# The gated heads' half of the output projection as seven block products instead of eight

## The chip, the cores and the metric

The kernel runs on one core of one Trainium2 chip. The metric is the device time of one execution in microseconds (us). The engines are TensorE (PE: matrix products, its weight loads are listed apart as PEld), VectorE (DVE), ScalarE (ACT), GpSimd (POOL) and SyncE (SP). PE writes to PSUM, eight banks of 128 x 512 float32; the others copy from there into SBUF. Transfers between SBUF and the chip's DRAM are issued by SP's queue or by POOL's queue and are carried by 16 DMA engines. Each engine takes its instructions strictly in the order of its own list.

## The reference, cut to what matters

A decoder layer on a sequence of 1024 rows, 1024 wide. After a norm the input is multiplied by `w_in`; eight heads of differential softmax attention give `oa` (1024 x 1024) and four heads of gated linear attention give `ob` (1024 x 1024). Each is normed and gated. Then comes the output projection:

```python
    ob = rms_norm(ob, gla_g).astype(x.dtype)
    ob = ob.reshape(B, S, GLA_WIDTH) * jax.nn.silu(gb)

    y = jnp.einsum('bse,ed->bsd', jnp.concatenate([oa, ob], axis=-1), w_out)
    return x + rms_norm(y, post_g)
```

`y` is therefore a sum of two products of 1024 x 1024 matrices: `oa` with the upper half of `w_out`, and `ob` (the gated heads' half) with the lower half. The change touches only how the second one is computed.

## The kernel before

**Precision.** Every float32 operand of a product is split into `hi` (rounded by a cast on ACT) and `lo` (the rest, by a subtraction on DVE), and each product is three matmuls: hi by hi, lo by hi, hi by lo. A split is thus one ACT and one DVE instruction on a 128 x 512 tile, and two transfers where the parts are stored.

**First stage, the input projection** (from the start to about 630 us). It already runs as seven products of blocks (`order`, steps (pair of columns, product number)); `go` takes one step after another: `prepare` splits the weights of the step that lies up to three steps ahead (`prepare(i + a)` for a = 0 to 3, into a ring of `NRING` = 5 tiles), `multiply` issues 12 matmuls (24 for wide ones), and `step` moves the sums on. Beside each step two things are worked off: `wo_step` loads one 128 x 512 tile of `w_out` (`wo_raw`), splits it (L584, L586) and stores the parts in DRAM (`wod`), 32 tiles in all; and from step (12, 5) on, `fill` advances `gla`, the gated heads, by one of its pieces. `gla` handles one head and half of the rows at a time (eight in all). Its last piece scales and gates the 2 x 128 x 512 result `o`, splits it at once and stores both parts in `mixe`.

**Second stage, attention and output projection** (about 630 to 925 us). `merge` interleaves three streams in the order of planned times: `all_scores` (scores and softmax, PE tile `sc`), `all_values` (transposes `wtr`, products `po`) and `out_early` (the output projection, PE tile `ypart`). What `merge` settles is the order of PE's list, which is pinned; the order on the other engines is a scheduler's. The loads of a head's keys and queries (`load_qk`, L875 and L878) are issued by SP when the head before has released the tiles.

`out_early` first makes the gated half: for each of 8 row tiles `st` and 2 column halves `dh`, 8 products of 128 x 128 x 512 over `e`, each three matmuls, that is 8 x 2 x 8 x 3 = 384 matmuls. ACT copies the sum from PSUM (`y_tile`, L1256) and SP stores it in DRAM (`yd`). The weights of this half, 16 tiles of 512 KB, are loaded once by POOL's queue before the stage starts (`weights(e)`, L910); the left sides come with `mix(st)`, two loads of 512 KB for each row tile. The last row tile waits until seven results of attention are stored. Then the first four attention heads' part is made in the same way, and POOL adds each sum to `yd` by an accumulating transfer (L1314).

**End** (from about 925 us): the last heads' part, the final norm and the stores.

Of the kernel before, what the change touches and what calls it, by code (L numbers as in the profile page):

```python
# [31 lines left out]
def hymba_kernel(  # L32
# [49 lines left out]
    gla_g = const.tile([P, 2], F32, name="gla_g")  # L82
# [15 lines left out]
    mixe = tc.dram_tile([NT, 2, P, 8, P], F32, name="mixe")  # L98
    wod = [tc.dram_tile([2, P, D], F32, name=f"wo{e}_d") for e in range(2 * D // P)]
# [84 lines left out]
    raws = {}  # L184

    def load_raw(p, halves=(0, 1)):
        if p >= len(pairs):
            return
        c0 = pairs[p][2]
        for kh in halves:  # L190
            if kh not in raws.setdefault(p, {}):
                r = ap.tile([P, HB, 256], F32, tag="raw", name="w_raw", bufs=4)
                rows = slice(kh * 512, kh * 512 + 512)
                sp.dma_start(r, w_in[0, rows, c0 : c0 + 256].rearrange("(k p) c -> p k c", p=P))
                raws[p][kh] = r
# [381 lines left out]
    wo_todo = [(e % 16, dh) for e in range(8, 24) for dh in range(2)]  # L577
    wo_open = []

    def wo_step(n):  # L580
        if n in (1, 6) and wo_open:
            e, dh, raw = wo_open.pop()
            hi = t_c("wo_hi", F32R)
            act.copy(hi, raw)  # L584
            lo = raw.bitcast(F32R)
            dve.tensor_tensor(lo, raw, fp(hi), ALU.subtract)  # L586
            for t, src in enumerate((hi, lo)):
                sp.dma_start(wod[e][t][:, cols(dh)], fp(src))
        if n in (2, 4) and wo_todo:
            e, dh = wo_todo.pop(0)  # L590
            raw = ap.tile([P, 512], F32, tag="t4", name="wo_raw", bufs=1)
            sp.dma_start(raw, w_out[0, e * P : (e + 1) * P, cols(dh)])
            wo_open.append((e, dh, raw))

    def go(n):
        for _ in range(n):
            i = made[0]
            if i == len(order):
                return
            made[0] = i + 1  # L600
            for a in range(4):
                prepare(i + a)
            step(i)
            if order[i][0] > EARLY and not (wide(order[i][0]) and order[i][0] % 2):
                wo_step(order[i][1])
            if fill and next(fill[0], 0) == 0:
                fill.pop(0)
# [114 lines left out]
    sp.dma_start(gla_g, gla_norm_g[0].rearrange("(t p) -> p t", p=P))  # L722
    lam4 = t_c("lam4").rearrange("p (a b) -> p a b", b=128)[:, :, :64]
# [19 lines left out]
    def gla_loads(g, half):  # L743

        if g < GLA_HEADS and (g, half) not in loaded:
# [3 lines left out]
            qd = kp.tile([P, 512], F32, tag="q1", name="gqd")  # L749
# [7 lines left out]

    def gla(g):

        u = None  # L760
        for half in range(2):
            cs = cols(half)
            kq, v, qd = gla_loads(g, half)
            gates = kp.tile([P, 2, 512], F32, tag="ks1", name="gg")
            yield
# [16 lines left out]
            act.copy(kn, pk)  # L782
            for t in range(2):
                sp.dma_start(gates[:, t], gg_d[g][t, :, cs])
            yield
            yield
            yield
            us = [u]
            for m in range(2):
# [8 lines left out]
                for i in range(min(2, NT - 1 - n)):  # L798
                    u1, u = u, ap.tile([P, 256], F32, tag="gu", name="gu", bufs=5)
# [46 lines left out]
            m_hi = gates.bitcast(F32R)  # L846
            for t in range(2):
                dve.scalar_tensor_tensor(
                    o[:, t], o[:, t], gla_g[:, t : t + 1], r, ALU.mult, ALU.mult
                )  # L850
                dve.tensor_tensor(o[:, t], o[:, t], gates[:, t], ALU.mult)
                act.copy(m_hi[:, t], o[:, t])
                m_lo = o[:, t].bitcast(F32R)
                dve.tensor_tensor(m_lo, o[:, t], fp(m_hi[:, t]), ALU.subtract)
                for i, src in enumerate((m_hi[:, t], m_lo)):
                    sp.dma_start(
                        mixe[half * 4 : half * 4 + 4, i, :, 2 * g + t, :].rearrange("s p c -> p s c"),
                        fp(src).rearrange("p (s c) -> p s c", c=P),
                    )
            yield  # L860

# [24 lines left out]
    fill.append(chain(*(gla(g) for g in range(GLA_HEADS))))  # L886
# [13 lines left out]
    def weights(e):  # L900
        i = e % 8
        wo[e] = [
            hw.tile(
                [P, D], F32R, tag=f"{('h11', 'h12', 's1', 'h22')[i // 2]}_{n}{i % 2}", name=f"wo_{n}"
            )
            for n in ("hi", "lo")
        ]
        engine = sp if e < E else pool
        for t in range(2):
            ins = engine.dma_start(fp(wo[e][t]), wod[e][t])  # L910
            if e >= E:
                tc.keep_in_program_order(ins)

    n_mix = [0]
# [8 lines left out]
    def mix(st):  # L923

        part = mix_tiles()
        for t in range(2):
            ins = sp.dma_start(fp(part[t]), mixe[st, t])
            if st < 2:
                tc.keep_in_program_order(ins)
        return part  # L930

    for e in range(E, E + 6):
        weights(e)
    go(2)
    mix0 = mix(0)
    go(3)
    weights(E + 6)
    weights(E + 7)
# [315 lines left out]
    def y_tile(ps):  # L1254
        y = smp.tile([P, 512], F32, tag="yst", name="yst", bufs=2)
        act.copy(y, ps)  # L1256
        return y

    def out_early():

        part = mix0
        ps = [y_bank(0, dh, "ypart") for dh in range(2)]
        for e in range(E, E + 8):
            yield 1.0
            if e == E:
                nxt = mix(1)
            for dh in range(2):
                times(ps[dh], part, E, dh, e, E + 7)
            yield 1.0
        for dh in range(2):  # L1270
            sp.dma_start(yd[0][dh], y_tile(ps[dh]))
        for st in range(1, NT - 1):
            part, nxt = nxt, mix(st + 1)
            rows = slice(ENDS[st - 1] * P, ENDS[st - 1] * P + P)
            sp.dma_start(out[0, rows, :], x[0, rows, :])
            for dh in range(2):
                ps = y_bank(st, dh, "ypart")
                for e in range(E, E + 8):
                    times(ps, part, E, dh, e, E + 7)
                    yield 0.69  # L1280
                sp.dma_start(yd[st][dh], y_tile(ps))

        yield lambda: len(stored) >= 7
        part = nxt
        ps = [y_bank(NT - 1, dh, "ypart") for dh in range(2)]
        raws_o = [load_mix(st, 0, 4) for st in ENDS[:3]]
        for e in range(E, E + 8):
            for dh in range(2):
                times(ps[dh], part, E, dh, e, E + 7)
                yield 0.69  # L1290
            if e < E + 4:
                weights(e - E)
            if e == E + 6:
                nxt = mix_part(ENDS[0], 0, 4, raws_o.pop(0))
        for dh in range(2):
            kept = sp.dma_start(yd[NT - 1][dh], y_tile(ps[dh]))
        for n, st in enumerate(ENDS):
# [11 lines left out]
            for dh in range(2):  # L1309
# [4 lines left out]
                pool.dma_start(yd[st][dh], y_tile(ps), accum_op=ALU.add)  # L1314
# [61 lines left out]
    def seed(st, dh, b, yp):  # L1376
# [3 lines left out]
        pin(b not in Y, act.copy(ps, yp))  # L1380

    def last_times(st, dh, part, e):
# [17 lines left out]
        [-6.0, T + LAG + 20, 16.0 + 14 * 5.52 + 16 * 2.76 + 11.8, out_early()],  # L1400
# [125 lines left out]
```

## Time and profile before

| | before |
|---|---|
| time, median of 3 runs (lowest to highest) | 980.24 us (978.34 to 980.25) |
| the profiled execution's own time | 979.08 us |
| its span, first to last instruction | 977.4 us |
| granted TensorE clock | 0.999 |
| busy: PE, DVE, ACT, POOL | 956.7, 735.4, 600.5, 142.9 us |
| moved by DMA | 220.45 MB, mean 226 GB/s |

A group line of the profile reads: source line, engine, operation, output tile <- input tiles, shape, xcount | busy us in all, mean ns of one | idle time of the engine just before them, and what ended it. A line of stages ("windows") reads: stretch in us, then for PE, PEld, DVE, ACT and POOL the busy us with the count of instructions, the granted clock, the mean busy share of the 16 DMA engines, and GB/s. In a list of waits the numbers are us in all, times, and the longest. The profile's DMA line for a queue gives packets, MB and the share of the 16 engines' time that its packets took.

### The profile page before, as it was taken

To read this page: it belongs to the slowest core of one execution; us is meant where nothing else is said; L and a number is where in the kernel's file an instruction comes from. 1 tells how busy PE (TensorE), PEld (TensorE's weight loads), DVE (VectorE), ACT (ScalarE), POOL (GpSimd) and SP (SyncE) were. 2 spreads that over 40 slices of the span, in tenths; PEclk is the share of its full clock that TensorE was granted. 3 is DMA by queue.
4 is the path that set the end of the run, shared out by engine and by line. 5 is a ranking of instruction groups with operands and counts; after the bars stand their busy time and mean duration, and the time that the engine had idled before them with its cause. 6 is when DMAs were issued, how large, how long until landed. Compare 5 with 4: busy or idle time off the path is not lost.

```text
span 977.4 us, 15766 instructions
## 1 busy us (share of the span) xinstructions
PE 956.7 (98%) x5338; PEld 830.4 (85%) x5338; DVE 735.4 (75%) x1452; ACT 600.5 (61%) x1164; POOL 142.9 (15%) x158
## 2 busy tenths in 40 slices
PE   5999999999999999999999999999999999999997
PEld 5998988888889998999888888878888888888785
DVE  6887597789866667686786876487888888898554
ACT  8742455487357455454665775366776687887773
POOL 4300000000000010000200002121322222443321
PEclk9999999999999999999999999999999999999999
DMA  9432446656774868897987866987656669994677
GB/s 345 151 110 91 139 135 205 231 179 225 238 247 162 264 187 286 254 294 229 293 259 243 273 202 191 407 269 272 197 186 228 240 199 344 340 294 105 151 208 147
DMA packets 152593, 220.45 MB, mean 226 GB/s; under 512 B 17104, under 2 KB 83664, under 8 KB 152416
## 3 DMA queue, kind: packets, MB, share of 16 engines
q1 hardware_dynamic: 146176, 203.71, 64.1%
q0 software_dynamic: 6336, 15.73, 7.0%
q8 instruction: 42, 0.69, 0.3%
q14 instruction: 39, 0.32, 0.1%
HBM read 133.93 MB, written 88.60 MB: 228 GB/s over the span
## 4 chain that ended last, share of the span: by engine, by line
PE 95%; DVE 2%; ACT 1%; DMA 1%; issue 1%; POOL 0%; SPq 0%; DVEq 0%; ACTq 0%; POOLq 0%
PE x L117 24%; PE y L117 15%; PE z L117 15%; PE ypart L117 13%; PE sc L117 7%; PE po L117 5%; PE yps L117 4%; PE wtr L120 3%; PE gpo L117 3%; PE kv L117 1%; PE gkl_ps L117 1%; PE pa L117 1%; DMA x<-in_x_dram 1%; PE xT L120 1%; DVE s_lo L548 0%
## 5 line engine op out<-in xcount | busy, mean ns | idle before, releaser
L315 ACT CAST w<-w_raw 128x512 fp32r<-128x512 f32 (+1 forms) x164 | 112.4, 688 | 94.7 <-PE y L117 44.1
L316 DVE TENSOR_TENSOR w<-w_raw,w 128x512 fp32r<-128x512 f32 (+1 forms) x164 | 126.7, 774 | 50.1 <-ACT w L315 43.3
L1049 ACT ACTIVATE p<-p,stt 128x896 f32<-128x896 f32 (+7 forms) x128 | 99.3, 777 | 36.7 <-DVE stt L1039 33.9
L427 ACT COPY s<-x 128x512 f32<-128x512 f32 x84 | 49.1, 585 | 84.4 <-PE x L117 84.3
L775 POOL TENSOR_SCALAR_AFFINE_SELECT gan<-gan 128x512 f32<-128x512 f32 x8 | 16.5, 2060 | 485.4 <-ACT gan L774 449.8
L296 DVE TENSOR_TENSOR w_raw<-w_raw 128x512 f32<-128x512 f32 (+1 forms) x96 | 75.9, 791 | 13.9 <-DMA w_raw<-in_w_in_dram 12.6
L1039 DVE CUSTOM_DVE_ANT_0 p<-sc,maskt 128x512 f32<-128x512 f32 (+3 forms) x128 | 74.3, 585 | 14.5 <-PE sc L117 13.3
L117 PE MATMUL ypart<-wo_hi,m_hi 128*128 128x512 f32 x192 | 79.5, 414 | 0.1
L117 PE MATMUL y<-h_hi,w 128*128 128x512 f32 x320 | 79.6, 391 | 0.0
L117 PE MATMUL z<-s_hi,w 128*128 128x512 f32 x320 | 79.6, 391 | 0.0
L117 PE MATMUL x<-s_hi,w 128*128 128x512 f32 x320 | 79.6, 391 | 0.0
L1055 POOL TENSOR_SCALAR p<-p,stt,lam 128x1024 f32<-128x1024 f32 (+3 forms) x64 | 56.2, 879 | 146.9 <-DVE stt L1054 141.9
L117 PE MATMUL ypart<-wo_hi,m_lo 128*128 128x512 f32 x192 | 75.5, 393 | 0.0
L117 PE MATMUL ypart<-wo_lo,m_hi 128*128 128x512 f32 x192 | 75.4, 393 | 0.0
L117 PE MATMUL sc<-k,q 128*128 128x512 f32 (+1 forms) x192 | 69.0, 363 | 1.3 <-DVE stt L1039 1.2
L117 PEld LDWEIGHTS x<-s_hi,w 128*128 128x128 f32 x320 | 59.7, 188 | 12.2
L117 PEld LDWEIGHTS y<-h_hi,w 128*128 128x128 f32 x320 | 59.6, 188 | 12.2
L117 PEld LDWEIGHTS z<-s_hi,w 128*128 128x128 f32 x320 | 59.5, 188 | 12.0
L117 PE MATMUL sc<-ks,q 128*128 128x512 f32 (+1 forms) x192 | 66.1, 347 | 0.0
L1097 ACT CAST wt_hi<-wtr 128x512 fp32r<-128x512 f32 (+1 forms) x80 | 42.7, 534 | 24.6 <-PE wtr L120 23.8
L1098 DVE TENSOR_TENSOR wt_lo<-wtr,wt_hi 128x512 fp32r<-128x512 f32 (+1 forms) x80 | 50.7, 633 | 8.6 <-ACT wt_hi L1097 8.0
L1058 DVE SCALAR_TENSOR_TENSOR p<-p,stt,p 128x1024 f32<-128x1024 f32 (+3 forms) x64 | 52.1, 814 | 4.1 <-POOL p L1055 3.9
(226 smaller groups left out, 2247.7 us busy)
## 6 DMA issues: line engine op xcount, KB each, us to landing
w_raw<-in_w_in_dram SPq DMA_DIRECT2D x56, 512.0 KB, 4.7
wo_raw<-in_w_out_dram SPq DMA_DIRECT2D x32, 256.0 KB, 3.0
wo_d<-wo_hi SPq DMA_DIRECT2D x32, 256.0 KB, 2.8
wo_d<-wo_raw SPq DMA_DIRECT2D x32, 256.0 KB, 3.8
q<-q_d SPq DMA_DIRECT2D x32, 256.0 KB, 4.7
k<-k_d SPq DMA_DIRECT2D x32, 256.0 KB, 5.7
ks<-k_d SPq DMA_DIRECT2D x64, 128.0 KB, 6.2
v<-v_d SPq DMA_DIRECT2D x16, 512.0 KB, 7.0
```

The costliest lines, as they stand in the source:

```text
L117: tc.keep_in_program_order(pe.matmul(*a, **k))
L120: tc.keep_in_program_order(pe.transpose(dst, src, ident))
L296: dve.tensor_tensor(dst, a, b, ALU.subtract)
L315: act.copy(w[0], src)
L316: dve.tensor_tensor(w[1], src, fp(w[0]), ALU.subtract)
L427: act.copy(b[k], ps)
L1039: ins = dve.tensor_tensor_reduce(p[:, a:e], sc[:, : e - a], maskt[:, NZ + P - (e - a) :] if last else maskt[:, : e - a], 1.0, 3e38 if i == ...
L1049: act.activation(p[:, :n], p[:, :n], AF.Exp, bias=st[:, m : m + 1], scale=-1.0, accum_out=st[:, 2 + m : 3 + m],)
L1055: pool.tensor_scalar(p1[:, :n], p1[:, :n], st[:, 5:6], lam, ALU.mult, ALU.mult)
L1058: dve.scalar_tensor_tensor(p0[:, :n], p0[:, :n], st[:, 4:5], p1[:, :n], ALU.mult, ALU.subtract)
L1097: act.copy(hi[:, :n], pt[:, :n])
L1098: dve.tensor_tensor(lo[:, :n], pt[:, :n], fp(hi[:, :n]), ALU.subtract)
```

## The change

Write the gated half as a product of 2 x 2 blocks of 512 rows or columns, left A (rows in two halves, columns by heads 0-1 and 2-3) and right W. Seven products of sums of blocks replace the eight products (the recipe that `order` uses in the input projection already). In detail:

- `out_early` runs over `U`, 28 entries (product n, row tile i of 128): each is 4 x 3 = 12 matmuls into a bank. Products 6 and 7 go on top of product 1 in the same bank, and 3 on top of 5, each after the bank has been copied out. That makes 28 x 12 = 336 matmuls.
- Each entry's bank is copied out by ACT: 28 copies. Sixteen of the results are stored in `yd` by SP, and sixteen are added to it by POOL's accumulating transfers (one entry of product 7 serves both).
- The four weight blocks that are sums are made in DRAM: SP copies a block of `w_out` to `wsd`, POOL adds another to it (16 copies, 16 accumulating transfers of 256 KB). `wo_step` splits 16 tiles of these beside 12 plain blocks and 16 tiles of the other half (before: 32 tiles), now one job every second step at most, with up to three raw tiles in flight; a spare half of the gated heads' `gqd` tile is one of them.
- The left sides that are sums are made in DRAM too (`lefts`): SP stores `o` (8 transfers of 512 KB), POOL adds (8 accumulating transfers). The split of `o` itself moves into the next piece (`gla_tails`) and is done for six of the eight results; 10 tiles of the sums are split by `wo_step`, and the last 6 by `late_left` beside the first products of the second stage.
- The left sides come in with one load of 512 KB for each entry (28 loads, four entries ahead); the weights of products 2, 4, 1 and 6 come by POOL's queue at the start (16 loads of 512 KB), those of 7, 5 and 3 by SP during the products (12 loads of 512 KB).
- Column half 1 of `y` is held with its sign turned, which `activation` with a scale undoes.

By the lists of instructions of the two kernels, PE has 5132 and 5084 instructions of products and transposes (48 fewer, all of them `ypart`, and the same order in the first stage), ACT 36 more, DVE 25 more, SP 124 more transfers to issue, POOL 40 more.

```diff
-    wo_todo = [(e % 16, dh) for e in range(8, 24) for dh in range(2)]
-    wo_open = []
+    wo_todo = [("block", n, k) for k in range(HB) for n in (2, 1, 3)]
+    wo_todo += [("sum", n, k) for k in range(HB) for n in (4, 6, 7, 5)]
+    wo_todo += [("rows", e, dh) for e in range(D // P) for dh in range(2)]
+    wo_todo += [("left", 7, k) for k in range(HB)]
+    wo_todo += [("left", n, k) for n in (5, 6, 3) for k in range(2)]
+    wo_open, wo_free, wo_now = [], {"t4": 0, "gup0": 0, "gup1": 0}, [0]
...
+                with tc.issue_after(last_raw[0]):
+                    sp.dma_start(wsd[n][k], src)
...
+    def add_weights(n, k, more):
+        pool.dma_start(wsd[n][k], more, accum_op=ALU.add, max_dma_last_dim=2048)
+        summed.add((n, k))
...
+    def wo_step():
+        now = wo_now[0]
+        wo_now[0] += 1
+        next(sum_steps, None)
+        if wo_open and wo_open[0][0] <= now - 3:
...
+            split(hi, lo, raw, -1.0 if (kind, n) in (("block", 2), ("left", 6)) else 1.0)
...
+            to = {1: (7, 6), 5: (5,), 2: (3,), 4: ()}[n]
+            for m in to:
+                sp.dma_start(lefts[m][g % 2].rearrange("t p c -> p t c"), o)
+            for m in {5: (7,), 4: (5,)}.get(n, ()):
+                pool.dma_start(
+                    lefts[m][g % 2].rearrange("t p c -> p t c"), o, accum_op=ALU.add
...
+    U = [(n, i) for i in range(4) for n in (2, 4)]
+    U += [(n, i + k) for i in (0, 2) for n in (1, 6, 7) for k in range(2)]
+    U += [(n, i + k) for i in (0, 2) for n in (5, 3) for k in range(2)]
...
     def out_early():
...
+        for j, (n, i) in enumerate(U):
+            if j == len(U) - 4:
+                yield lambda: len(stored) >= 7
+                raws_o = [load_mix(st, 0, 4) for st in ENDS[:3]]
+            load_left()
+            if j == 0:
+                load_left()
+            late_left(j)
+            for k, m in ((8, 7), (10, 5), (16, 3)):
+                if j in (k, k + 1):
+                    gla_weights(m, halves=(j - k,))
+            if 20 <= j < 24:
+                weights(j - 20)
...
+            ps = held[{6: 1, 7: 1, 3: 5}.get(n, n), i]
+            for k in range(HB):
+                hi, lo = wg[n][k // 2]
+                m = lefts_in[j]
+                for a, (u, v) in enumerate(((0, hi), (1, hi), (0, lo))):
...
+            y = y_tile(ps)
+            for st, dh, add in {
+                2: ((i, 0, False),), 4: ((4 + i, 0, False),), 1: ((i, 0, True),),
+                6: ((i, 1, False),), 7: ((4 + i, 0, True), (4 + i, 1, False)),
+                5: ((4 + i, 1, True),), 3: ((i, 1, True),),
+            }[n]:
+                if add:
+                    pool.dma_start(yd[st][dh], y, accum_op=ALU.add)
+                else:
+                    kept = sp.dma_start(yd[st][dh], y)
...
-        [-6.0, T + LAG + 20, 16.0 + 14 * 5.52 + 16 * 2.76 + 11.8, out_early()],
+        [-6.0, T + LAG + 20, 16.0 + 24 * 2.76 + 16 * 2.76 + 11.8, out_early()],
```

More of the change, by code (lines that the diff above doesn't have):

```diff
@@ L1252, in y_bank, with y_tile @@
         return bank(Y[dh], [P, 512], name)
[L1254 removed]
+    def y_tile(ps, sign=1.0):
         y = smp.tile([P, 512], F32, tag="yst", name="yst", bufs=2)
[L1256 to L1296 removed]
```

264 lines of the change are left out of this document (205 added, 59 removed).

## Prediction

> **What bounds the kernel now.** I read the page first: busy times, the row of slices, the chain that ended last.
>
> ```profile
> span 977.4 us, 15766 instructions
> PE 956.7 (98%) x5338; PEld 830.4 (85%) x5338; DVE 735.4 (75%) x1452; ACT 600.5 (61%) x1164; POOL 142.9 (15%) x158
> ...
> PE   5999999999999999999999999999999999999997
> ...
> DMA  9432446656774868897987866987656669994677
> ...
> PE 95%; DVE 2%; ACT 1%; DMA 1%; issue 1%; POOL 0%; SPq 0%; DVEq 0%; ACTq 0%; POOLq 0%
> ```
>
> PE is busy in every slice but the first and the last, and 95% of the chain is PE. A busy PE may hide waits, so next the list of PE's waits from 150 to 925 us. It has a single line:
>
> ```profile
> PE sc L117 <- DVE stt L1039: 1.2, 2, 0.9
> ```
>
> In 775 us PE waits 1.2 us for others. A matmul that is removed there shortens the kernel by its own issue time, as long as nothing else becomes late. That issue time comes from the chain in order of time (start, length, what), once in each stage; the group line of `ypart` stands beside it:
>
> ```profile
> 212.72 2.72 PE z L117 x12
> ...
> 635.73 1.36 PE ypart L117 x6
> ...
> L117 PE MATMUL ypart<-wo_hi,m_hi 128*128 128x512 f32 x192 | 79.5, 414 | 0.1
> ```
>
> Twelve matmuls of 512 columns take 2.72 us and six take 1.36 us: 227 ns each. The 414 ns of the group line is the length of one matmul that overlaps its neighbours; it is no price.
>
> The rest of the argument rests on stages (stretch, PE, PEld, DVE, ACT, POOL busy us, clock, share of the DMA engines, GB/s):
>
> ```profile
> 150.00:600.00 450.00, 450.00 (x2528) 394.58 (x2527) 336.40 (x523) 260.80 (x457) 16.48 (x8) 1.00 0.73 235
> 610.00:635.00 25.00, 24.89 (x110) 20.30 (x109) 11.32 (x19) 7.80 (x13) 3.70 (x7) 1.00 1.03 407
> 633.00:804.00 171.00, 169.76 (x898) 143.63 (x897) 140.85 (x393) 121.43 (x267) 43.48 (x47) 1.00 0.70 227
> 800.00:875.00 75.00, 74.96 (x401) 63.63 (x400) 65.38 (x176) 60.12 (x130) 26.69 (x29) 1.00 1.01 327
> 633.00:925.00 292.00, 290.72 (x1541) 246.31 (x1540) 238.81 (x645) 214.73 (x467) 87.55 (x94) 1.00 0.76 238
> ```
>
> Two things are to be seen. The DMA engines are the second most loaded resource, at 0.70 to 0.76 over long stretches. And from 800 to 875 us they are full (1.01) while PE still works 74.96 of 75 us: full queues alone do not stop PE.
>
> **Part 1, matmuls.** 384 become 336: 48 x 0.227 = 10.9 us less on PE's list, all in the second stage and all before the point where `out_early` waits for the seventh stored result (before it there were 7 x 48 = 336, now 24 x 12 = 288). In the first stage PE's order is unchanged. This is the only saving.
>
> **Part 2, splits and copies.** Their prices, by group:
>
> ```profile
> L584 ACT CAST wo_hi<-wo_raw 128x512 fp32r<-128x512 f32 x32 | 19.8, 619 | 37.4 <-DMA wo_raw<-in_w_out_dram 27.0 <-issue 3.4 <-DMA v_d<-c 2.6
> L586 DVE TENSOR_TENSOR wo_raw<-wo_raw,wo_hi 128x512 fp32r<-128x512 f32 x32 | 22.0, 688 | 23.3 <-ACT wo_hi L584 16.4 <-DMA q_d<-c 5.5 <-DMA v_d<-v_hi 1.3
> ...
> L1256 ACT COPY yst<-ypart 128x512 f32<-128x512 f32 x32 | 18.5, 579 | 5.8 <-PE ypart L117 5.4
> ...
> L1314 POOL DMA_DIRECT2D y_d<-yst x16 | 14.2, 885 | 25.4 <-ACT yst L1256 20.2 <-DVE stt L1054 5.1
> ```
>
> First stage: 54 tiles split by `wo_step` for 32, and 12 halves of `o` for 16, so 18 splits more: 11.1 us on ACT (18 x 0.619), which is busy 261 of 450 us, and 12.4 us on DVE (336 of 450). Second stage: 6 splits and 12 copies more, 3.7 + 6.9 = 10.6 us on ACT and 4.1 us on DVE. With PE 10.9 us shorter, DVE has 243 of 281 us, 86%; from 800 to 875 us it has 65.38 of 75, 87%, and PE does not wait. I take nothing for these. The cover is the order: weights are split up to three steps ahead, 3 x 2.72 = 8.2 us; a hold-up of ACT or DVE beyond that lands on PE one for one. POOL gets 16 accumulating issues more in the second stage, 16 x 0.885 = 14.2 us beside 87.55 of 292. What stands behind each in POOL's list is the softmax scaling of the next block, and it waits as long as the issue waits for ACT's copy (20.2 us over 16 issues before). Scores run a head ahead of values, so I take nothing here either.
>
> **Part 3, transfers.** This is the doubtful term. Prices from the DMA lines: first the plain queue from 633 to 804 us; then POOL's queue from 834 to 925 us, where it carries only the 16 accumulating transfers; then a stretch of 16 us (818 to 834) with full queues and the ordinary mix.
>
> ```profile
> DMA packets 17992, 38.88 MB, mean 227 GB/s; under 512 B 2394, under 2 KB 2394, under 8 KB 17978
> ...
> q0 software_dynamic: 2160, 3.93, 27.7%
> ...
> DMA packets 2589, 5.30 MB, mean 331 GB/s; under 512 B 271, under 2 KB 783, under 8 KB 2589
> ...
> q1 hardware_dynamic: 2589, 5.30, 94.3%
> ```
>
> An accumulating transfer of 256 KB takes 0.277 x 91 / 16 = 1.58 us of all engines. Plain transfers run at full load between 331 / 0.943 = 351 GB/s (ordinary mix) and 407 GB/s (610 to 635 us, mostly 512 KB loads).
>
> First stage: 38 loads and copies of 256 KB, 44 stores more for the splits and 8 fewer for `o`, 8 stores of 512 KB: 23.6 MB, 58 to 67 us; and 16 + 8 accumulations worth 8.4 MB, 32 x 1.58 = 51 us. The stage leaves 0.27 x 450 = 122 us free. It fits with 4 to 13 us to spare. A transfer inside DRAM that accumulates has no row; I use the price from SBUF, the nearest. As the loads have slack, I take 0 and keep a loss of up to 15 us as a rival.
>
> Second stage up to the wait (171 us before): 12 more left loads of 512 KB, 12 weight loads of 512 KB, 6 late loads and 12 late stores of 256 KB, 17.3 MB; and 12 of the 16 accumulations, 18.9 us. With the 38.9 MB that are there, 56.2 MB take 138 us at 407 GB/s and 160 at 351, so 157 to 179 us with the accumulations. PE needs 171 - 10.9 = 160. At one end all is hidden, at the other PE is held up 19 us. The added loads are like those at the fast end, those that are there like the slow one, so I go by the middle, 379 GB/s: 148 + 18.9 = 167 us, which is 7 us more than PE.
>
> Where that shows first: a head's keys are loaded late, in one burst. SP's issues before the seventh head, that head's first 512-column score on PE, and the landing time (median) of its `ks` loads:
>
> ```profile
> 820.27 0.32 SPq L875 DMA_DIRECT2D k<-k_d  x1
> ...
> 823.46 3.84 SPq L878 DMA_DIRECT2D ks<-k_d  x4
> ...
> 832.30 0.45 PE L117 MATMUL sc<-k,q 128*128 128x512 f32 x1
> ...
> ks<-k_d SPq DMA_DIRECT2D x4, 128.0 KB, 6.6
> ```
>
> The last `ks` is issued by 827.3 us and lands within some 6.6 us; PE wants it at 832.3. With full queues nothing is left of the margin, and the change fills the queues for the heads before that, too. PE's list being in order, a late key stops everything.
>
> **Sum.** 979.08 (the profiled execution) - 10.9 + 7.1 = 975.3, say 975.5 us. The profiled execution lies 1.2 us under the median of the three runs, 980.24, within their scatter of 1.9; I leave it.
>
> **The rivals.**
>
> *All hidden.* The transfers move at the fast rate: 979.08 - 10.9 = 968.2 us. For it: 1.01 from 800 to 875 us cost PE nothing. Against it: that lasted two heads, this lasts five. Chance 0.20.
>
> *The transfers bound the second stage.* At the slow end PE is held up 179 - 160 = 19 us at the head boundaries: 979.08 - 10.9 + 19 = 987 us. It decides from about 370 GB/s downwards, where the hold-up exceeds 10.9 us by then (56.2 MB in 152 us). For it: the ordinary mix shows 351, and the loads of the `rows` weights (8 x 0.52 MB) now also begin before the wait, which would add up to 12 us, 999 at worst. Against it: left sides are loaded four entries ahead, weights earlier still, so part of it can slip behind. Chance 0.28.
>
> *A ceiling on bytes to and from DRAM.* If DRAM traffic and not engine time is limited, an accumulation counts twice (it reads and writes its target): 56.2 + 6.3 = 62.5 MB. At the 351 GB/s of the ordinary mix that is 178 us, 18 us over PE, 986 us. Against it: the row at 407 GB/s. Chance 0.05. The Trainium skill, DMA: Bandwidth & Descriptors, section "Where 436 GB/s comes from", says that between HBM and SBUF the HBM side binds at about 358 GB/s for one core; by that figure it would be an estimated 175 us, and 983 us in all. The trace has 407 GB/s over 25 us, so here the measurement speaks against the rule.
>
> *Loads late in the first stage.* Waits of ACT for `wo_raw`, from the list of waits:
>
> ```profile
> ACT wo_hi L584 <- DMA wo_raw<-in_w_out_dram: 27.0, 12, 7.9
> ```
>
> ACT already waits once for 7.9 us, with the weights of later steps behind it, against a cover of 8.2. With 54 jobs and full queues some waits pass it: five times 3 us would be 15 us, 979.08 - 10.9 + 15 = 983 us. Chance 0.08.
>
> *A matmul is worth its 414 ns.* 48 x 0.4 = 19 us, 960 us. The 12 in 2.72 us speak against it. Chance 0.02.
>
> **How the numbers follow.** The forecast has 0.37; its own range is 970 to 981, of which 0.26 is faster by over 0.2% (under 978.3) and 0.11 within 0.2%, about what a measurement of this kernel can tell from no change. Faster: 0.26 + 0.20 + 0.02 = 0.48; same 0.11; slower 0.28 + 0.05 + 0.08 = 0.41. The range for 8 in 10, 966.5 to 989, leaves out the last rival, the edges of the first and the worst of the second.
>
> **What would show it.** `ypart` with 48 matmuls fewer and still 227 ns apart; DMA share of 0.95 or more from 633 to 800 us; PE waits of `sc` for `k`, `ks` or `q` at the boundaries of heads two to six, 5 to 10 us in all; no PE waits from 150 to 600 us. I am wrong if PE has no DMA waits there (968), or if they exceed 11 us, or if PE waits for `w` in the first stage.

## Result, and the profile after

The changed kernel takes 1021.88 us (median of four runs, 1021.06 to 1026.06) beside 980.22 us for the kernel before: 1.0439 times as long, interval 1.0427 to 1.0451. The forecast was 975.5 us with a range up to 989.0. It was wrong by 46 us, and in its sign.

The page of the kernel after: busy times, the slices of PE and of the DMA engines, and the shares of the chain that ended last.

```profile
span 1020.5 us, 16063 instructions
PE 965.7 (95%) x5290; PEld 831.4 (81%) x5290; DVE 749.1 (73%) x1477; ACT 618.6 (61%) x1200; POOL 174.5 (17%) x198
...
PE   6999999889999999999998999969899899999997
...
DMA  9343369998985988998999989999999999985667
...
PE 47%; DMA 29%; DVE 10%; ACT 7%; issue 4%; SPq 2%; POOL 0%; DVEq 0%; ACTq 0%; POOLq 0%
```

PE issues 48 matmuls fewer and is busy longer, since its busy time counts slow matmuls too (the granted clock is 0.981 over the span, before 0.999). Of the 43.1 us that the span is longer, 34.1 are idle time of PE (54.8 us beside 20.7) and 9.0 are busy time, where 10.9 us less had to be expected. The chain, 95% PE before, is now 47% PE and 29% DMA. The DMA row, which went up and down between 4 and 9 in the first stage from 150 us on, stands at 8 or 9 nearly everywhere from 150 to 900 us.

The list of PE's waits over the whole kernel (us in all, times, longest; the 8.8 us at its start and the small ones left out) names no single culprit:

```profile
PE ypart L127 <- DMA m_in<-mixe: 7.3, 1, 7.3
PE x L127 <- ACT s L440: 7.0, 5, 2.8
PE sc L127 <- DMA ks<-k_d: 3.5, 2, 2.4
PE gpo L127 <- DVE gu L918: 2.5, 1, 2.5
PE sc L127 <- DVE stt L1203: 2.2, 2, 1.9
PE gms L127 <- DVE sq_hl L952: 2.0, 2, 1.7
PE ms L127 <- DVE wt_lo L1262: 2.0, 2, 1.6
```

Where the time goes is seen better from the same matmul in both traces. The table gives how much later it starts than in the kernel before, in us, worked out from PE's list of each trace: three matmuls of the input projection (at 248, 504 and 612 us of the kernel before), the first score of the second and of the fifth head, and the first matmul of the end. The experiments told below are in it, except e12 and e16. Kernels whose first stage has the same edits (after, e4, e7, e10, e15, e17) differ there by up to 2.8 us (8.1 to 10.9 at 248 us, 24.8 to 26.9 at 612), so a difference of 2 or 3 us in this table decides nothing.

| kernel | 248 | 504 | 612 | head 2 (656) | head 5 (762) | end (924) | median us |
|---|---|---|---|---|---|---|---|
| after | 9.9 | 15.3 | 24.8 | 33.3 | 35.2 | 43.3 | 1021.9 |
| e1 before, 48 matmuls fewer | 0.1 | 0.4 | 0.4 | 4.2 | 0.2 | -3.2 | 975.9 |
| e3 before + weight sums | 13.6 | 16.6 | 16.6 | 16.7 | 16.7 | 16.5 | 996.7 |
| e5 the same, spread | 9.3 | 22.4 | 22.4 | 22.5 | 22.9 | 23.1 | 998.9 |
| e13 e5, loads further ahead | 5.0 | 7.9 | 7.9 | 7.9 | 7.9 | 7.7 | 988.9 |
| e2 after, no weight sums | -0.7 | 5.2 | 19.3 | 27.3 | 29.1 | 38.0 | 1016.8 |
| e8 after, no left sums | 10.2 | 11.9 | 16.8 | 27.1 | 29.2 | 36.8 | 1014.3 |
| e4 after, no y additions | 10.7 | 17.2 | 26.6 | 35.3 | 36.4 | 33.0 | 1011.4 |
| e9 after, no sums at all | 0.4 | 4.2 | 7.8 | 19.5 | 20.2 | 16.8 | 995.9 |
| e18 e9, late splits queued behind | -1.1 | 1.1 | 5.6 | 15.0 | 13.9 | 10.9 | 992.0 |
| e11 after, weight splits later | 7.6 | 21.0 | 32.6 | 51.7 | 52.4 | 57.8 | 1037.3 |
| e14 after, splits not waiting | 16.1 | 21.3 | 34.6 | 43.8 | 46.3 | 55.7 | 1032.6 |
| e19 after, ACT halves from a constant | 12.7 | 17.2 | 27.1 | 37.2 | 39.0 | 46.7 | 1025.3 |
| e7 after, m_in earlier | 10.9 | 16.4 | 26.8 | 38.7 | 40.2 | 46.2 | 1022.7 |
| e10 e7, late splits later | 9.3 | 14.1 | 26.9 | 38.9 | 39.6 | 48.1 | 1025.6 |
| e15 e7, late splits not waiting | 9.5 | 14.2 | 26.1 | 37.2 | 40.0 | 40.7 | 1019.2 |
| e17 e10, late splits queued behind | 8.1 | 14.6 | 25.5 | 35.9 | 39.0 | 45.6 | 1026.5 |

So the change lost 25 us in the first stage, 8 at the passage into the second, and 10 more up to the end, the saved matmuls already taken off. How full the DMA engines were is in the windows: the first stage of both kernels, before first, then the second stage of the kernel after from its first score on (the kernel before has 0.70 there, in the prediction's rows; the last three columns are clock, DMA share, GB/s):

```profile
150.00:612.00 462.00, 462.00 (x2581) 404.52 (x2580) 342.10 (x531) 266.11 (x466) 22.29 (x19) 1.00 0.73 235
```

```profile
150.00:637.00 487.00, 471.72 (x2581) 408.97 (x2580) 352.21 (x548) 275.13 (x483) 40.09 (x44) 0.99 0.93 290
657.00:830.00 173.00, 156.40 (x787) 129.65 (x786) 132.07 (x361) 117.00 (x252) 48.88 (x53) 0.95 1.04 347
```

The first stage went from a share of 0.73 to 0.93, the second from 0.70 to 1.04. What a fuller queue means for those who wait is in the lines of the DMA issues from 150 to 600 us, whose last number is the median time from issue to landing. Before:

```profile
wo_d<-wo_hi SPq DMA_DIRECT2D x32, 256.0 KB, 2.8
...
wo_raw<-in_w_out_dram SPq DMA_DIRECT2D x31, 256.0 KB, 2.9
gq_d<-c SPq DMA_DIRECT2D x16, 256.0 KB, 2.6
...
q_d<-c SPq DMA_DIRECT2D x22, 128.0 KB, 3.0
```

After:

```profile
wg_d<-wo_hi SPq DMA_DIRECT2D x28, 256.0 KB, 5.1
...
wo_raw<-in_w_out_dram SPq DMA_DIRECT2D x19, 256.0 KB, 5.6
gq_d<-c SPq DMA_DIRECT2D x16, 256.0 KB, 6.1
...
q_d<-c SPq DMA_DIRECT2D x22, 128.0 KB, 5.6
```

Loads and stores alike take 1.8 to 2.3 times as long to land as before. A store holds its tile until it lands, and `wo_hi` and the sums `c` that leave PSUM share four tiles.

One place shows the whole way to PE. ACT's waits from 176 to 192 us, then PE's own list at 183 us, then the clock in the 4 us after:

```profile
ACT wo_hi L646 <- DMA wg_d<-wo_raw: 6.4, 1, 6.4
```

```profile
182.73 1.07 PE L127 MATMUL y<-h_hi,w 128*128 128x512 f32 x4
183.64 1.07 PE L127 MATMUL y<-h_lo,w 128*128 128x512 f32 x4
187.47 3.42 PE L127 MATMUL x<-s_hi,w 128*128 128x512 f32 x8 [2.76 <-ACT s L440]
190.74 0.63 PE L127 MATMUL x<-s_lo,w 128*128 128x512 f32 x2
```

```profile
188.00:192.00 4.00, 4.00 (x14) 3.13 (x13) 2.65 (x4) 0.60 (x2) 0.81 (x1) 0.71 1.10 254
```

ACT stands 6.4 us in front of a split of weights until a store has landed. The line names a store of `wo_raw`, but by the trace that one landed only at 184.6 us, after the split had begun (183.7). What landed just before is a store `gq_d<-c`, issued at 174.3 us and 9.3 us on its way, one of those that hold a tile of the four. Behind the split in ACT's list is, after a second split that waits 1.5 us more, the copy `s` of a sum out of PSUM. PE needs that bank, waits 2.76 us, and then needs 3.27 us for eight matmuls (187.47 to 190.74), 409 ns each instead of 227: the granted clock has dropped, to 0.71 on average in these 4 us.

### The profile page after: what moved, and what is told of

Its sections match the earlier page's. It is cut to its first block, busy times and chain, and to the rows that moved or that the text cites. A ratio compares the mean times of both kernels' runs of the same rounds, so it can differ in the third digit from the quotient of the medians.

```text
span 1020.5 us, 16063 instructions
## 1 busy us (share of the span) xinstructions
PE 965.7 (95%) x5290; PEld 831.4 (81%) x5290; DVE 749.1 (73%) x1477; ACT 618.6 (61%) x1200; POOL 174.5 (17%) x198
## 2 busy tenths in 40 slices
DMA packets 187475, 273.96 MB, mean 268 GB/s; under 512 B 19728, under 2 KB 98576, under 8 KB 187296
## 3 DMA queue, kind: packets, MB, share of 16 engines
q0 software_dynamic: 13120, 28.32, 14.1%
## 4 chain that ended last, share of the span: by engine, by line
PE 47%; DMA 29%; DVE 10%; ACT 7%; issue 4%; SPq 2%; POOL 0%; DVEq 0%; ACTq 0%; POOLq 0%
PE x L127 10%; PE ypart L127 8%; PE z L127 6%; PE y L127 6%; PE sc L127 5%; PE yps L127 4%; DMA wo_raw<-in_w_out_dram 4%; PE po L127 3%; DMA w_raw<-in_w_in_dram 3%; PE wtr L130 2%; DMA left_d<-go 2%; DMA wg_d<-wo_hi 2%; DVE w L329 2%; DMA q_d<-c 1%; DMA m_raw<-mixd 1%
## 5 line engine op out<-in xcount | busy, mean ns | idle before, releaser
L1213 ACT ACTIVATE p<-p,stt 128x896 f32<-128x896 f32 (+7 forms) x128 | 99.2, 776 | 36.4 <-DVE stt L1203 35.1
L127 PE MATMUL x<-s_hi,w 128*128 128x512 f32 x320 | 83.1, 403 | 7.0 <-ACT s L440 7.0
L127 PE MATMUL ypart<-wg_hi,m_in 128*128 128x512 f32 x224 | 75.0, 417 | 9.1 <-DMA m_in<-mixe 7.3
L1261 ACT CAST wt_hi<-wtr 128x512 fp32r<-128x512 f32 (+1 forms) x80 | 42.7, 537 | 25.1 <-PE wtr L130 22.5
L127 PEld LDWEIGHTS ypart<-wg_hi,m_in 128*128 128x128 f32 x224 | 40.5, 197 | 14.7 <-issue 7.7
L127 PE MATMUL po<-wt_hi,v 128*128 128x512 f32 (+1 forms) x192 | 50.7, 349 | 1.5 <-ACT o L1356 1.5
L130 PE MATMUL wtr<-ident,p 128*128 128x128 f32 x288 | 45.5, 276 | 2.8 <-DVE wt_lo L1262 1.7
```

The source lines that it names most:

```text
L127: tc.keep_in_program_order(pe.matmul(*a, **k))
L130: tc.keep_in_program_order(pe.transpose(dst, src, ident))
L1213: act.activation(p[:, :n], p[:, :n], AF.Exp, bias=st[:, m : m + 1], scale=-1.0, accum_out=st[:, 2 + m : 3 + m],)
L1261: act.copy(hi[:, :n], pt[:, :n])
```

## The experiments

Theories: T1, the transfers fill the queues, so that what others wait for lands late. T2, the added splits and copies stand in the way in ACT's and DVE's lists. T3, the sums inside DRAM do harm by themselves. T5, formed after the first runs: what holds PE is a split that stands in the list before a load that has not landed. (The saving's own price is e1.) Ratios below are to the kernel before, timed on the same chip.

**e1, the saving alone.**

```diff
         for i, (a, b) in enumerate(((mh, hi), (ml, hi), (mh, lo))):
+            if i == 2 and E <= e < E + 3:
+                continue
```

> The kernel before, with 48 of its 384 ypart matmuls left out (the third term of three of the eight row tiles; all transfers and splits stay). This is the change's saving alone. Theory that the saving is real and the loss lies elsewhere: 980.2 - 48 x 0.227 = 969.3 us. Rival, that PE's matmuls in the second stage hide waits so that fewer of them buy less: over 975 us.

By its edit the kernel leaves out the third matmul of three of the eight products over `e`, in every bank of the gated half.

975.92 us, ratio 0.9962 (0.9948 to 0.9976): 3.7 us gained, not 10.9, as the rival had it. PE's waits and two windows of this run:

```profile
PE ypart L117 <- DMA m_hi<-mixe: 2.3, 1, 2.3
...
PE ypart L117 <- DMA m_lo<-mixe: 0.7, 1, 0.7
```

```profile
650.00:655.00 5.00, 1.97 (x9) 1.29 (x8) 3.05 (x11) 3.07 (x8) 1.64 (x2) 1.00 0.92 358
655.00:660.00 5.00, 5.00 (x25) 4.34 (x24) 3.12 (x11) 3.02 (x10) 0.66 (x1) 0.66 1.06 290
```

From the second head on it gains 7.4 us (4.2 to -3.2 in the table). But at 650 us PE now waits for the second left tile, and the clock falls to 0.66 after it. In the kernel before nothing waited there, with the same transfers: SP issued that tile's loads at 642.5 us, here at 647.3. The passage from the first to the second stage had no slack. That the lists were planned anew around a shorter PE may be why the loads moved; it was not tried.

**e3 and e2, the weight sums put into the kernel before, and taken out of the kernel after.** e3 adds `weight_sums` and its steps to the kernel before; e2 is:

```diff
-                with tc.issue_after(last_raw[0]):
-                    sp.dma_start(wsd[n][k], src)
...
-        pool.dma_start(wsd[n][k], more, accum_op=ALU.add, max_dma_last_dim=2048)
...
-            return wsd[n][k]
+            return w_block(*{4: (1, 0), 5: (0, 1), 6: (1, 1), 7: (1, 1)}[n], k)
```

> The kernel before plus the 32 transfers that form the sums of weight blocks, paced as in the changed kernel, one a step; nothing uses them. T1: its stage has 0.27 of the engines free, so they cost little alone, 980 to 984 us, the loss needs the added loads and stores as well. T2: 980 us. T3: 25 us of loss come with them alone, about 1005 us.

> The changed kernel without the 16 copies inside DRAM and the 16 accumulating transfers that form the sums of weight blocks; the tiles of the sums are loaded from single blocks of w_out instead, so the sums are left out, and every split, store and matmul stays. Theory T1 (too many bytes at once: stores and loads land late and hold ACT's and DVE's tiles): PE's delay of 9.9 us against before that arises from 171 to 250 us goes, the later 15 us of the first stage stay for the most part: about 1010 us. Theory T2 (the splits themselves, queued among ACT's and DVE's other work, hold PE): no change, 1020 to 1023 us. Theory T3 (the sums are the whole loss of the first stage): 1022 - 25 = 997 us.

e3: 996.72 us, 1.0172 (1.0155 to 1.0189). 32 transfers whose results nothing uses cost 17 us, 13.6 of them by 248 us. That lies between the marks of T1 (980 to 984) and T3 (1005) and bears out neither. PE waits there, and ACT from 150 to 640 us:

```profile
PE z L120 <- DVE c L446: 7.3, 1, 7.3
PE x L120 <- ACT s L433: 4.7, 3, 3.1
```

```profile
ACT wo_hi L622 <- DMA wo_raw<-in_w_out_dram: 36.5, 14, 7.3
...
ACT wo_hi L622 <- DMA ws_d<-in_w_out_dram: 10.1, 1, 10.1
```

No split was added, so T2 cannot explain it. e2: 1016.79 us, 1.0368 (1.0344 to 1.0393). The 9.9 us up to 248 us are gone, as T1 said, but 19.3 of the 24.8 are there again at 612 us, so T1's 1010 is missed too. T3, that the weight sums are the whole loss of the first stage, falls for the changed kernel.

**e8 and e4, the left sums and the y additions taken out.** e8 drops the stores to `lefts` and the accumulations into them and loads those tiles from `w_out`; e4:

```diff
-                if add:
-                    pool.dma_start(yd[st][dh], y, accum_op=ALU.add)
-                else:
+                if not add:
```

> The changed kernel without the transfers that form the left sums (the stores of o to the lefts and the accumulations into them; the tiles to be split are loaded from blocks of w_out instead, so these sums are left out), every split, load, store of split tiles and matmul kept. T1: the 15 us that PE loses from 350 us to the end of the first stage go for the most part: 1008 to 1012 us. T2 (the added splits in ACT's and DVE's order): 1020 to 1023 us.

> The changed kernel without the 16 accumulating transfers that add products of blocks to the stored y tiles (that part of the sum is left out; the copies out of PSUM and all matmuls stay). T1: 16 x 1.58 = 25 us of engine time leave the second stage, whose PE lost 20 us there; two thirds or more of it comes back, 1002 to 1008 us. T2 (copies and splits in ACT's order): no change, 1020 to 1023 us.

e8: 1014.29 us, 1.035 (1.0332 to 1.0367): from 248 us to 612 us the loss is 6.6 us instead of 14.9. e4: 1011.37 us, 1.0318 (1.0296 to 1.034): from the second head to the end PE gains 2.3 us where the changed kernel loses 10.0. Sixteen transfers, 25 us of the DMA engines' time by the prediction's price, are worth 12 us of PE. In both runs less came back than T1 had expected (1008 to 1012 and 1002 to 1008). In e2 and e8 the loads of the sums' tiles also no longer wait for the sums. That weighs little: from 150 to 640 us SP's list in the kernel after stands some 7 us in all behind transfers of the sums.

**e9, none of these sums.** The edits of e2, e8, e4 and e7 together.

> The changed kernel without weight sums, without left sums and without the 16 y additions (all of these sums are left out), and with the third and fourth left tile loaded early; all splits, stores of split tiles, loads, copies out of PSUM and matmuls stay. T1: 25 us of the first stage, 8 of the start and 10 of the heads come back, what is left being the added plain loads: about 980 us, between 976 and 988. T2 (splits and copies hold PE): above 1005 us.

995.87 us, 1.0157 (1.0139 to 1.0175). The first stage's loss falls from 24.8 to 7.8 us though every split and copy is still there: T2 falls as the main cause. The share of the DMA engines is 0.83 there:

```profile
150.00:600.00 450.00, 445.00 (x2496) 389.22 (x2495) 340.96 (x530) 265.00 (x465) 14.50 (x8) 1.00 0.83 268
```

It missed its 980 because these 7.8 us stay and the passage still costs 11.7 us (7.8 to 19.5).

**e5 and e13, spread, and loaded further ahead.** In the kernel before; e13 on top of e5 gives the weight tile two buffers in turn until the gated heads start.

```diff
-                next(sum_steps, None)
+                spread[0] += 1
+                if spread[0] % 3 == 0:
+                    next(sum_steps, None)
...
-        if n in (1, 6) and wo_open:
+        if n in (1, 6) and len(wo_open) > deep[0]:
```

> The kernel before plus the same 32 transfers for sums of weight blocks, but one copy and one accumulation every third step instead of every step. Theory T1, read as a rate: at one pair a step the pairs alone want (0.7 + 1.6 us of all DMA engines) per step of 2.72 us, 0.84 on top of the 0.63 that the stretch had; every third step 0.28, so 0.91 to 0.95 in all: it nearly fits, and 13 of the 17 us that the dense version cost go: 980 to 985 us. Rival T3 (an accumulation inside DRAM holds up whatever shares the queues, however far apart): the same 997 us.

> The kernel before plus the 32 spread transfers for weight sums, which cost 19 us, but with the split of a weight tile one load later (two tiles in turn instead of one, up to the first gated head; same transfers and splits otherwise). T5: the 19 us came from ACT standing before wo_hi for a tile on its way (65 us of waits in that run, 27 in the kernel before); with the load a further 3 steps ahead they go: 980 to 985 us. Rival T3 (accumulations inside DRAM slow every transfer, whatever the order): 995 us or more.

e5: 998.9 us, 1.0186 (1.0164 to 1.0209). Spreading buys nothing, and the reading of T1 as a rate falls; T3's mark of 997 was met. e13: 988.9 us, 1.0092 (1.0069 to 1.0115): half of it back with the same bytes. ACT's wait in front of the split, from 150 to 640 us, in e5 and in e13 (27.0 in the kernel before):

```profile
ACT wo_hi L623 <- DMA wo_raw<-in_w_out_dram: 65.3, 19, 9.7
```

```profile
ACT wo_hi L623 <- DMA wo_raw<-in_w_out_dram: 27.7, 11, 7.0
```

In the kernel before, then, the distance from a load to its split, with the second tile that it takes, decides about half of the loss. The rest stays although ACT's wait is back at its old level: 988.9 lies between the marks of T5 (980 to 985) and T3 (995 or more). T3 is not the whole, and T5 was the theory to test in the changed kernel.

**e11, the same idea in the changed kernel.**

```diff
-        if wo_open and wo_open[0][0] <= now - 3:
+        if wo_open and wo_open[0][0] <= now - (5 if len(wo_free) > 1 else 3):
```

> The changed kernel with each weight tile split five steps after its load instead of three, as long as there are three tiles for it (to about 300 us); the same transfers, splits and sums. T5: ACT's waits for wo_raw from 160 to 250 us go, and PE's delay of 9.9 us there with them; the rest stays: 1011 to 1015 us. T1 (the queues are over-full there, share 1.05): the delay is only put off by the five steps and comes back, 1019 to 1023 us.

1037.28 us, 1.0581 (1.0563 to 1.0599), a miss on both theories. Up to 248 us it is 2 us better, no more than the scatter, and then worse everywhere: tiles kept longer mean fewer jobs done while there are three tiles (17 splits by 300 us instead of 22), and more of them later, beside the gated heads. Together with e10's edits it took 1045.87 us, 1.0679 (1.0661 to 1.0697):

> Both of these edits together. T5: they add up, 1001 to 1005 us. T1: 1019 to 1023 us.

**e14 and e19, splits that wait for no load.** e14 lets the splits read a constant tile, with an additional tile of the four `c` for the second half. e19 does without that tile:

```diff
-            hi, lo = t_c("wo_hi", F32R), raw.bitcast(F32R)
-            split(hi, lo, raw, -1.0 if (kind, n) in (("block", 2), ("left", 6)) else 1.0)
+            hi = t_c("wo_hi", F32R)
+            act.copy(hi, maskt[:, :512])
...
-            for t, src in enumerate((hi, lo)):
+            for t, src in enumerate((hi, hi)):
```

> The changed kernel in which the first stage's splits of weight and left tiles read a constant tile that is always there; the tiles are still loaded, and as many bytes are stored, so that the transfers are the same, but no split waits for a load (the values of the gated heads' weights are left out). T5 (ACT and DVE stand in their order before a tile that has not landed): most of the 25 us that PE loses in the first stage goes: 998 to 1005 us. T1 (full queues make stores, the tiles they hold and the projection weights late): at most a few us, 1016 us or more.

> The changed kernel in which the first stage's weight and left splits are only ACT's half, copied from a constant tile and stored twice (DVE's half and the values are left out): every load and store is there, with the same four c tiles, and nothing waits for a load. T5 (splits that wait for loads hold PE): the first stage's 25 us go for the most part: 998 to 1006 us. T1 (stores that land late hold the c tiles and the projection's own loads are late): 1014 us or more.

e14: 1032.63 us, 1.0535 (1.0498 to 1.0571), worse, and no test, as the waits moved to the `c` tiles that it takes twice as many of. e19: 1025.29 us, 1.0449 (1.0421 to 1.0477), as T1 had it, and 27.1 us lost in the first stage: T5 falls as the main cause in the changed kernel, and T2 once more, since DVE has 33 us less to do from 150 to 600 us (294.17 against 327.39). One reservation: both stores of a split now read the `c` tile, which is held until the second has landed, and a gain may be used up there. What its ACT and DVE wait for instead, from 150 to 640 us:

```profile
ACT w L328 <- DMA w_raw<-in_w_in_dram: 13.8, 3, 8.2
...
ACT wo_hi L666 <- DMA wg_d<-wo_hi: 12.6, 9, 4.3
```

```profile
DVE w_raw L309 <- DMA w_raw<-in_w_in_dram: 21.6, 5, 6.7
...
DVE sq L949 <- DMA v_d<-c: 8.9, 2, 6.0
...
DVE c L424 <- DMA v_d<-c: 7.6, 3, 3.2
```

These are the projection's own weights (`w_raw`) and stores that hold `c` tiles. Take away one thing that waits for a transfer and the next one waits: T1, read as landing times.

**e7, e10, e15 and e17, the passage into the second stage.** e7 loads the left tiles three and four early; e10 also makes the late splits three entries after their load, e15 lets them read a constant, e17 queues them on ACT behind a later copy:

```diff
-    load_left()
-    load_left()
+    for _ in range(4):
+        load_left()
...
-        if late_open:
+        if late_open and late_open[0][3] <= j - 3:
...
+            with tc.issue_after(last_y[0]):
+                split(hi, lo, raw, -1.0 if n == 6 else 1.0)
```

> The changed kernel with the third and fourth left tile (m_in) loaded together with the first two, ahead of the last stores of the first stage, not behind them. Theory that the 8.4 us lost at the start of the second stage come from SP's order (the load issued at 665.8 us behind 13 stores that wait for the last sums, landing at 672.1): 1022 - 7.5 = 1013 to 1015 us. Rival, that the load is late since the queues are full: the earlier load lands late too or pushes the keys, 1020 us or more.

> The changed kernel with the third and fourth left tile loaded early (as in the run before, where nothing was gained) and the late splits of left sums done three entries of the list of products after their load instead of one. Theory T5 (what holds PE is a split that stands in ACT's and DVE's fixed order behind a load that has not landed: in the run before, ACT's left_hi waited 11.4 us for its tile and the scores' minima behind it on DVE waited 9.9): the 9.7 us that PE then waited go, with 1.5 us of clock after the gap: 1011 to 1014 us. T1 (bytes): the bytes are the same, 1022 us.

> The changed kernel with the third and fourth left tile loaded early, and the six late splits of the second stage reading a constant tile while their loads and stores go on (the values of these left sums are left out). T5: the 9.7 us at the second head's first scores, which stayed in both runs that touched this place, go, with the clock after the gap: 1010 to 1013 us. T1: 1020 us or more.

> The changed kernel with the third and fourth left tile loaded early, and each late split queued on ACT behind the copy of a later product out of PSUM, some 10 us after its place before; same transfers. If the 9.5 us at the second head's first scores are the price of that place in ACT's and DVE's order: they go, with 1.5 us of clock: 1010 to 1014 us. If full queues at that point hold PE in any order (keys, m_in): 1019 to 1025 us.

1022.74, 1025.56, 1019.22 and 1026.47 us: nothing gained beyond the scatter, and each time 10 to 12 us at the same place. In e7, e10 and e15 PE waits there once, 9.5 to 10.0 us, for the softmax on DVE (`stt`). What DVE and ACT waited for, in e7, e15 and e17:

```profile
DVE left L650 <- ACT left_hi L649: 9.9, 1, 9.9
```

```profile
DVE left_lo L650 <- DMA left<-left_d: 9.6, 1, 9.6
```

```profile
ACT yst L1421 <- DMA y_d<-yst: 8.6, 2, 6.7
```

First the left tile `m_in` (in the kernel after), then the split of a late tile, then a tile of the same four buffers (e15 takes two of them for each split), then one of the two `yst` tiles whose store had not landed. SP comes to these transfers only when it has issued the 24 stores of the last projection steps (646.8 to 664.2 us in the kernel after, up to 668.5 in e17). The transfers that it issues in the next 10 us take 3.5 to 8.7 us to land, and the products now want a new 512 KB left tile every 12 matmuls, where before a pair of them served 48.

**e18, no sums, and the late splits behind.** e9 with e17's edit. e16 (e14 and e15 together, without the y additions) took 1021.72 us and shares their flaws; T5's 982 was missed.

> The kernel without any sums (995.9 us, its late splits' values left out too) with the late splits queued behind as well. It keeps the added plain loads, stores and splits alone. If the place in the order was the price of the start: 995.9 - 11 = 985 us, 983 to 988; then the seven products would not beat the kernel before (980) even with sums for nothing. If the queues hold PE there anyway: 993 to 998 us.

> The two edits together, and without the 16 y additions. T5: 1022 - 20 - 10 - 10 = 982 us, between 976 and 990; all sums' transfers, loads and stores of the first stage are still there. T1: above 1000 us.

e18: 991.95 us, 1.0127 (1.011 to 1.0144), between its two marks: the passage costs 9.4 us instead of 11.7, a difference within the scatter. Even with every sum for nothing the seven products are 12 us behind the kernel before. The second stage, from 5 us before its first score, is nearly as full as with them:

```profile
633.00:804.00 171.00, 160.50 (x821) 133.41 (x820) 135.71 (x369) 120.08 (x259) 38.60 (x42) 0.97 1.01 353
```

No version tried beats the kernel before, except e1, which only leaves work out.

## Why the prediction was wrong, point by point

- **What bounds the kernel.** Right for before. The sentence that full queues alone do not stop PE, taken from 75 us at a share of 1.01, did not carry over to 173 us at 1.04, where the keys of a head and the products' tiles came late (PE busy 156 of 173 us).
- **Part 1, 10.9 us.** The price of 227 ns held: from the second head to the end e1 issues 39 matmuls fewer, 8.9 us by that price, and gains 7.4. Its "as long as nothing else becomes late" did not: e1 kept 3.7 us.
- **Part 2, splits at 0.** Right for most of the first stage's loss: e9 and e19 show that it did not come from the added splits. In the second, e4 keeps every copy and split and gets 12 us back. The cover named for them, three steps or 8.2 us, was the wrong one: it covers weights, while the copies of sums out of PSUM stand behind the same splits with no cover but the next free bank.
- **Part 3, first stage at 0: the step that failed.** The sum itself held: share 0.73 of 462 us before is 337 us of all DMA engines, 0.93 of 487 us after is 453, so 116 us were added where 109 to 118 had been counted. The moved bytes also came out, 273.96 - 220.45 = 53.5 MB, which is what the prediction's items add up to. What was wrong is the conclusion "it fits, so it costs nothing". At 0.93 the engines had room, but landing times doubled (2.6 to 6.1 us for `gq_d<-c`), and lists in fixed order wait for landings. The stage cost 25 us; the loss of up to 15 us had been kept as a rival at 0.08. That rival had the path wrong as well: it and the sign named for it spoke of late weights, but from 150 to 640 us PE waited 0.8 us for `w` and 7.0 for the copies `s` out of PSUM.
- **Part 3, second stage at 7.1 us.** The bytes up to the wait and the rate were both mis-sized. From 657 to 847 us the kernel after does what the kernel before does from 633 to 804 (the sixth head's first score moved from 797 to 839 us). Plain transfers moved 60.6 MB in 92.3% of these 190 us: 175 us at 345 GB/s, where the forecast had 148 us for 56.2 MB at 379. The accumulations took 9.5%, 18 us, as forecast. Eight loads of the `rows` weights (4.2 MB, issued from 784 to 807 us) did begin before the wait, as the rival "the transfers bound the second stage" had feared. From the second head to the end PE issued 42 matmuls fewer (9.5 us) and lost 10.0 us more all the same, so it was held up some 19.5 us there, and 29.1 from the first score on, with the passage told next; the rival had 179 - 160 = 19, and up to 12 more for these loads.
- **What was in no case:** the passage, 8.5 us in the changed kernel, 8 to 12 in its variants (e11 and e12: 18 to 19), 3.8 even in e1. The prediction quoted the loads before the seventh head as the tight place and did not use SP's list at 630 to 645 us. Nor has it a term for the clock: by the means over the span (0.981 of 1020.5 us, 0.999 of 977.4) its drops cost up to some 18 us, an estimate, as part of them falls into waits.
- **The DRAM ceiling.** From 657 to 847 us plain transfers moved 345 GB/s beside the accumulations and 346 without them (e4: 63.4 MB in 96.4%). A limit on bytes that counts an accumulation twice would have let the plain rate rise. The Trainium skill, DMA: Bandwidth & Descriptors, section "Where 436 GB/s comes from", has 358 GB/s for one core from HBM, and the stage's mean of 347 lies just below it; but the kernel before ran at 407 over 25 us (the prediction's row), so the figure is no ceiling here.
- **The sum.** 25.1 (delay at the first score of all) + 9.6 (8.2 at the passage and 1.4 for six matmuls saved before it) + 19.5 - 10.9 = 43.3 us, the delay at the end in the table. The clock's drops are in these numbers.

Shown: the sums' transfers made 17 of the first stage's 25 us, y additions 12 of the second stage's. Open: how the remaining 6 to 8 us of the first stage are shared out, how much of all this is SP's longer list (124 transfers more to issue) and not the transfers themselves, and which of the things that are late at the passage would have to be early for PE to run through; four edits moved the wait without shortening it.

## What to carry to other kernels

A sum of transfer times that fits into the free time of the queues is only half of an estimate: look up landing times beside the share, and for each engine's list what stands behind a wait for a landing. Ask of every tile pool how long a store may hold a tile before the next user waits, since removing one waiter only shows the next. And price a saving on PE by leaving the work out, before building what is to replace it: here that run would have said 3.7 us.

## What the runs showed of the hardware

- **The clock falls after short waits.** In the kernel after PE waited 2.0 us at 211 us, 7.3 at 672 and 2.4 at 801, and the windows after these read:

```profile
211.00:215.00 4.00, 4.00 (x12) 3.13 (x11) 3.84 (x5) 0.09 (x1) 1.13 (x2) 0.60 1.08 292
672.00:676.00 4.00, 3.76 (x10) 3.12 (x11) 1.27 (x5) 1.15 (x3) 0.00 (x0) 0.50 1.06 391
801.00:805.00 4.00, 4.00 (x11) 3.14 (x12) 2.58 (x6) 2.24 (x4) 0.88 (x1) 0.57 1.04 407
```

  At 187 us, after a wait of 2.76, eight matmuls took 3.27 us instead of 1.8, so such a wait can cost about 1.5 us more than its length. After 1.25 and 1.5 us (375 and 612 us) the clock stayed at 1.00, and so it did after 2.0 and 2.3 us in e18 (380 and 549 us): the length of the wait alone does not decide. The Trainium skill, TensorE: Matmul & The Clock Gate, section "Part 1: The HAM clock gate", puts the drop to half clock after an idle window of about 3.4 us; the half agrees with 0.50, the length does not: 2.0 us were enough here.
- **Accumulating inside DRAM takes the DMA engines about as long as from SBUF.** POOL's queue in the kernel after, from 150 to 600 us, where it carries only accumulating transfers, most of them inside DRAM:

```profile
q0 software_dynamic: 3664, 6.82, 9.4%
```

  9.4% of 450 us for 6.82 MB are 6.2 us for each MB; the accumulations from SBUF in the prediction's row took 6.4 (27.7% of 91 us for 3.93 MB). From 150 to 300 us, where all of them are inside DRAM, it is 5.9 (16.6% of 150 us for 4.20 MB).
